# First block of a diffusion layer's projections: modulation sums on VectorE alone, side work tied behind the last convolution, value bounds by maxima

## The chip, the cores and the metric

The kernel runs on one core of a Trainium2 chip. The core has five engines with a queue each: TensorE (PE, with its weight loads as PEld), VectorE (DVE), ScalarE (ACT), GpSimd (POOL) and SyncE (SP), which issues the DMAs. Each engine works through its queue in the order in which the program was laid down. The metric is device time in microseconds: the median before is 2546.75 us (three runs, 2542.22 to 2547.43).

## The reference

One layer of a backbone works on 128 context tokens and 2048 latent tokens of width 1024. What matters here is the front part of it:

```python
def modulation(cond, w_mod_l, b_mod_l):
    m = jax.nn.silu(cond) @ w_mod_l + b_mod_l
    return jnp.split(m[:, None, :], N_MOD, axis=-1)
...
    h = rmsnorm(x, norm_mix_l) * (1.0 + sc1) + sh1
    proj = h @ w_in_l
    qkv = jax.nn.silu(centred_conv(qkv, conv_l))
    q, k, v = jnp.split(qkv, 3, axis=-1)
    q = l2norm(q.reshape(B, T, H_A, DK))
    k = l2norm(k.reshape(B, T, H_A, DK))
```

The six parts of the modulation have 1024 columns each, for two conditions (context and latent). The first two are needed at once; the others are needed after the projections. Behind this part come the delta-rule scans, the gated MLP, the output projection, the feed-forward part and the final norm.

## The kernel before

**Tiles and blocks.** The 17 token tiles of 128 are taken in six blocks: five of three tiles, the last of two. In each block twelve feature tiles are projected, in the order of four key heads (gi 1), four query heads (gi 0) and four value heads (gi 2). A feature tile is eight rows of 128 input features times three matmuls (`mm3`, lines 297 to 299), since weights and tokens are split into a high and a low half of 16 bits. `convolve` (lines 637 to 642) then makes the three-tap convolution and the silu of it: a copy on ACT (637), two multiply-adds on DVE (639), tanh on ACT (641), one more multiply-add on DVE (642). `to_tokens` transposes the result on PE (651) and takes norms on ACT (668, 672); `to_features` transposes keys back (681) and evicts them (682), `products` multiplies keys and queries (692).

**Weights and their powers.** Before a weight group may be split into halves (`split16`, ACT 205 and DVE 206), a power of two is needed that bounds its values. For the keys it comes from a maximum of absolute values on DVE (`largest`, 219). For queries and values it comes from sums of squares on ACT (`squares`, 248, with a read of the accumulator), and `group_power` then takes the maximum (253) and calls `powers`: transpose on PE (224), maximum (226), product with the identity (228), a matmul with ones that spreads it over the partitions (229), a copy (232), the power -1/2 on POOL (234) if the input was squared, a mask of the exponent (235), a scale and a reciprocal (237, 238 or 240, 241). `group_ready` scales the taps (873), and then the splits of that group can begin.

**Modulation sums.** `mods` holds the steps of the later six column groups (jc 4 to 9, eight steps each). For jc 4, `split_mod_steps` splits each fetched row block (ACT 198, DVE 199) and sums on PE with two matmuls per step against `cW` (456, 457). For the others, `mod_steps` keeps two accumulators on DVE (325 for the first step, 327 after it), and `total` adds over partitions with eight small matmuls on PE (336) and four adds (342).

**Order.** A scheduler lays the instructions down on each engine by its own estimate of when each is ready, so that a step written late may be laid down early. `behind` and `in_turn` add an order for ACT and DVE alone: the instructions of a step come after those of a named earlier step. For `mods` the named step is the modulation step before it, and at first the splits of the key weights; nothing holds them behind the convolutions that are written ahead of them. `late` does not exist yet. Side work is dealt into the feature tiles by `interleave`: splits of query weights in tiles 0 and 1, value rows `w1_raw(2, k)` in tiles 0 to 3 with their squares, value splits in tiles 4 to 7, rows and columns of the next block (`prep_block`; ACT 540 for the rows' squares, DVE 597 and 600 for the columns), and from block 2 on the rows and splits of the next weight groups.

## Time and profile before

The profiled execution took 2547.12 us, of which the span from the first to the last instruction is 2545.4 us; the 1.7 us around it are not in the trace.

| | value |
|---|---|
| median of the runs | 2546.75 us |
| the profiled execution | 2547.12 us |
| its span | 2545.4 us |
| PE busy | 2492.7 us (98%) |
| DVE busy | 1857.0 us (73%) |
| ACT busy | 1278.6 us (50%) |
| mean granted TensorE clock | 0.993 |

How to read it: a view of windows gives the busy time of each engine in a stretch, with the granted TensorE clock (1.00 is full, 0.50 half). A row of the timeline gives the start, the length, the engine, the line, the operation, what it writes and reads, how often, and in brackets the idle time before it and what ended it. Records of matmuls overlap: one of 128x388 is recorded as 0.33 us while the next starts 0.16 us after it.

### The profile page before, as it was taken

The numbers are of one execution on the slowest core, as the hardware profiler recorded it, in microseconds if no ns is written. First come the engines' busy times: TensorE is split into PE (matmuls) and PEld (weight loads), VectorE is DVE, ScalarE is ACT, GpSimd is POOL, SyncE is SP. The second block draws the span as 40 slices with busy tenths as digits, with TensorE's granted clock in tenths as the row PEclk, the third lists the DMA queues.
The fourth block names the chain that finished last, engine by engine and source line by source line (L and its number), as shares of the span: only waits on it lengthen the run. The fifth ranks groups of instructions, "written<-read, shape, count | busy, mean of one in ns | idle before, by whom it ended". The sixth has DMA issues, their size and how long they took to land.

```text
span 2545.4 us, 44002 instructions
## 1 busy us (share of the span) xinstructions
PE 2492.7 (98%) x15150; PEld 1915.7 (75%) x15150; DVE 1857.0 (73%) x3861; ACT 1278.6 (50%) x3157; POOL 237.4 (9%) x429
## 2 busy tenths in 40 slices
PE   8899999999999999999999999999999999999998
PEld 3466568566666688888888888888888888888887
DVE  4856878777777888986687877777765557784875
ACT  3765665555555667763455544444343433243442
POOL 3111223211111111210000000000000000000000
PEclk9899999999999999999999999999999999999999
DMA  8754755644444657885877789655489979786673
GB/s 284 259 179 142 223 168 174 201 148 133 140 137 148 196 175 248 289 280 174 292 235 234 247 292 336 194 174 175 140 280 375 339 251 327 252 262 205 226 262 108
DMA packets 479334, 566.61 MB, mean 223 GB/s; under 512 B 37684, under 2 KB 284764, under 8 KB 475526
## 3 DMA queue, kind: packets, MB, share of 16 engines
q1 hardware_dynamic: 479110, 563.80, 67.8%
q8 instruction: 119, 1.95, 0.3%
q14 instruction: 105, 0.86, 0.1%
HBM read 392.90 MB, written 170.76 MB: 221 GB/s over the span
## 4 chain that ended last, share of the span: by engine, by line
PE 81%; DVE 8%; DMA 6%; ACT 2%; SPq 1%; issue 1%; POOL 1%; POOLq 0%; DVEq 0%; ACTq 0%
PE f L297 16%; PE f L299 16%; PE f L298 15%; PE pj L297 6%; PE pj L298 6%; PE pj L299 6%; PE pd L1127 5%; PE pm L297 1%; PE pm L299 1%; PE pm L298 1%; PE pt L692 1%; DMA raw<-in_w_ff_dram 1%; DMA raw<-in_w_mod_dram 1%; DMA QK<-qk_d 1%; PE pt L651 1%
## 5 line engine op out<-in xcount | busy, mean ns | idle before, releaser
L297 PE MATMUL f<-hop,zH 128*128 128x512 f32 (+1 forms) x976 | 376.2, 386 | 1.2 <-ACT zH L1649 1.2
L299 PE MATMUL f<-hop,zL 128*128 128x512 f32 (+1 forms) x976 | 376.2, 386 | 0.4 <-DVE zL L1643 0.4
L298 PE MATMUL f<-hop,zH 128*128 128x512 f32 (+1 forms) x976 | 376.1, 386 | 0.0
L297 PE MATMUL f<-hop,wH 128*128 128x512 f32 x896 | 349.7, 391 | 3.0 <-DMA hop<-hop_d 1.5
L298 PE MATMUL f<-hop,wH 128*128 128x512 f32 x896 | 348.7, 389 | 0.0
L299 PE MATMUL f<-hop,wL 128*128 128x512 f32 x896 | 347.3, 389 | 0.0
L1649 ACT CAST zH<-zraw 128x512 fp32r<-128x512 f32 x240 | 146.3, 620 | 291.5 <-DMA zraw<-s_d 87.0
L1643 DVE TENSOR_TENSOR zL<-zraw,zH 128x512 fp32r<-128x512 f32 x240 | 162.5, 687 | 72.4 <-ACT zH L1649 52.7
L297 PEld LDWEIGHTS f<-hop,zH 128*128 128x128 f32 x976 | 183.3, 188 | 38.6 <-ACT zH L1649 1.8
L299 PEld LDWEIGHTS f<-hop,zL 128*128 128x128 f32 x976 | 183.3, 188 | 38.3 <-DVE zL L1643 1.3
L298 PEld LDWEIGHTS f<-hop,zH 128*128 128x128 f32 x976 | 183.3, 188 | 36.8 <-issue 0.2
L297 PEld LDWEIGHTS f<-hop,wH 128*128 128x128 f32 x896 | 168.2, 188 | 38.7 <-ACT p L1722 2.3
L299 PEld LDWEIGHTS f<-hop,wL 128*128 128x128 f32 x896 | 168.2, 188 | 35.3
L298 PEld LDWEIGHTS f<-hop,wH 128*128 128x128 f32 x896 | 168.3, 188 | 34.5
L298 PE MATMUL pj<-kL,w 128*128 128x386 f16 (+2 forms) x568 | 182.0, 323 | 0.8 <-DVE kL L600 0.7
L297 PE MATMUL pj<-kH,w 128*128 128x386 f16 (+2 forms) x568 | 181.7, 323 | 1.1 <-DVE cv L639 0.5
L299 PE MATMUL pj<-kH,w 128*128 128x386 f16 (+2 forms) x568 | 180.4, 321 | 0.0
L181 POOL TENSOR_TENSOR r<-rsq,nhalf 128x1 f32<-128x1 f32 (+1 forms) x37 | 25.3, 683 | 1388.5 <-DVE rsq L180 1388.5
L1649 ACT CAST wH<-s 128x512 fp32r<-128x512 f32 x96 | 59.4, 621 | 123.3 <-DVE s L1643 116.4
L639 DVE SCALAR_TENSOR_TENSOR cv<-pj,vec,cv 128x384 f32<-128x384 f32 (+2 forms) x142 | 83.2, 590 | 42.2 <-ACT cv L637 40.8
L297 PE MATMUL pj<-w,hrow 128*128 128x512 f16 x248 | 94.0, 379 | 0.0
L298 PE MATMUL pj<-w,hrow 128*128 128x512 f16 x248 | 94.0, 379 | 0.0
(456 smaller groups left out, 5547.2 us busy)
## 6 DMA issues: line engine op xcount, KB each, us to landing
zraw<-z_d SPq DMA_DIRECT2D x212, 256.0 KB, 4.4
raw<-in_w_ff_dram SPq DMA_DIRECT2D x192, 256.0 KB, 5.1
hop<-hop_d SPq DMA_DIRECT2D x28, 1024.0 KB, 9.6
z_d<-c SPq DMA_DIRECT2D x96, 256.0 KB, 4.7
zraw<-s_d SPq DMA_DIRECT2D x96, 256.0 KB, 5.3
raw<-in_w_mod_dram SPq DMA_DIRECT2D x80, 256.0 KB, 3.1
r<-in_w_ff_dram SPq DMA_DIRECT2D x80, 256.0 KB, 5.1
s_d<-s SPq DMA_DIRECT2D x64, 256.0 KB, 3.1
```

The source lines that it names most:

```text
L181: G.tensor_tensor(out=out, in0=t[:np_, :n], in1=nhalf[:np_, :n], op=ALU.pow)
L297: T.matmul(ps, lh, rh, start=first and i == 0, stop=False, skip_group_check=more)
L298: T.matmul(ps, lh, rl, start=False, stop=False, skip_group_check=more)
L299: T.matmul(ps, ll, rh, start=False, stop=last and i == n - 1, skip_group_check=more)
L639: V.scalar_tensor_tensor(out=cv, in0=ps[:, w : w + ncol - 2], scalar=convw[:, w, j : j + 1], in1=cv, op0=ALU.mult, op1=ALU.add)
L651: T.transpose(pq[:, i * P : (i + 1) * P], u["x2"][i], ident)
L692: T.matmul(ps[:, i * P : (i + 1) * P], kTt[:, i * P : (i + 1) * P], rhs[i], start=True, stop=True)
L1127: T.matmul(p[:, h, :], lhs[:, h, :], rhs[:, h, :], start=True, stop=True)
L1643: V.tensor_tensor(out=out, in0=a, in1=b, op=op)
L1649: A.copy(h, src)
```

## The change

Six edits:

- All 48 modulation steps are made by `mod_steps`; `split_mod_steps` and `cW` are gone. The accumulators come from the pool `p1`.
- The value rows no longer have squares on ACT: `squares` takes their largest absolute value on DVE, and `powers` for that group runs without the power on POOL. For inputs that are not squared the copy ahead of the mask is gone too, and the mask reads PSUM.
- `late` ties the ACT and DVE instructions of a step behind those of the convolution that was written last (`done["conv"]`). It is used for the value rows with their maxima, the rows of the next block, the rows of the later weight groups with their squares, and the modulation steps.
- The tables that need the first powers (lines 862 to 868 before) are written as a step behind the last column of the first block.
- Eight matmuls with ones (`keep_warm`), which stood at the start alone, are issued at two more places of the head: after the last first-half modulation output, and after the first `powers`.
- Keys of the first block are evicted on DVE, where ACT did it.

```diff
-        V.tensor_copy(ef, ps[:, P : P + n])
         if squared:
+            V.tensor_copy(ef, ps[:, P : P + n])
             G.tensor_tensor(out=ef, in0=ef, in1=nhalf[:, 0:n], op=ALU.pow)
-        V.tensor_scalar(out=e[:, 0:n], in0=e[:, 0:n], scalar1=0x7F800000, scalar2=None, op0=ALU.bitwise_and)
+        V.tensor_scalar(out=e[:, 0:n], in0=e[:, 0:n] if squared else ps[:, P : P + n].bitcast(I32), scalar1=0x7F800000,
+                        scalar2=None, op0=ALU.bitwise_and)
...
+        if gi == 2:
+            largest(phase[gi][:, k : k + 1], raw)
+            return
...
-        powers(power[:, i : i + 1], under[:, i : i + 1], top, 1, psum, True)
+        powers(power[:, i : i + 1], under[:, i : i + 1], top, 1, psum, gi != 2)
...
+        def keep_warm():
+            warm = pt()
+            for _ in range(WARM):
+                T.matmul(warm[:, 0:P], ones, ones, start=True, stop=True)
...
+                start = here()
...
+                done["conv"] = tc.nc.cur_bb.bb.instructions[start:]
...
-                (V.tensor_copy if bi else A.copy)(kTt[:, :n], pk[:, :n])
+                V.tensor_copy(kTt[:, :n], pk[:, :n])
...
-        mods = [st for jc in range(4, 10) for st in (split_mod_steps(jc) if jc == 4 else mod_steps(jc, pe))]
+        mods = [st for jc in range(4, 10) for st in mod_steps(jc, p1)]
...
         mod_out(r3, 1, a1, vec[:, 8:16], True)
+        keep_warm()
...
         powers(st3[:, 0:3], st3[:, 3:6], tops, 3, pt)
+        keep_warm()
...
+        in_turn("tables", tables, "column")
...
+        def late(f):
+            start = here()
+            f()
+            behind("conv", start, both)
...
-                done["mods"] = done["split"]
+                done["conv"] = done["split"]
...
-                    side += [lambda k=k: wv.append(w1_raw(2, k)) for k in range(2 * n, 2 * n + 2)]
+                    side += [lambda k=k: late(lambda: wv.append(w1_raw(2, k))) for k in range(2 * n, 2 * n + 2)]
...
-                        side.append(lambda w=w, k=n: load_w2(w, k))
+                        side.append(lambda w=w, k=n: late(lambda: load_w2(w, k)))
...
-                    side += [lambda f=f: in_turn("mods", f, "mods") for f in mods[:1]]
+                    side += [lambda f=f: late(f) for f in mods[:1]]
...
-                    side += nxt[1][n - 2 : n - 1] if bi == 0 and n >= 2 else nxt[1][n : n + 1] if bi else []
+                    side += [lambda f=f: late(f) for f in (nxt[1][n - 2 : n - 1] if bi == 0 and n >= 2 else
+                                                           nxt[1][n : n + 1] if bi else [])]
```

Line numbers shift with it. In the changed kernel `mm3` is 301 to 303, `convolve` 615, 617, 619 and 620, the norms of `to_tokens` 647 and 651, the transposes of token rows 564, the columns 574 and 577, the key eviction 661, a modulation step 329 and 331, its total 340 and 346; 205, 206, 219, 224 to 229 and 235 stay.

Three places show how the queues move. The first is PE at the end of the head, from the last output of the first modulation sums (431 before, 434 now) to the first projection; 224 and 229 are the transpose and the spreading matmul of `powers`, 587 or 564 the transposes of token rows. Before:

```order
L431 MATMUL pm<-ident,first 128x2 x4
L224 MATMUL pt<-ident,tops 3x128
L587 MATMUL pt<-ident,x 128x128 x3
L229 MATMUL pt<-topd,ones 128x3
L712 LDWEIGHTS abW
L712 MATMUL pm<-kH,abW 32x388
L297 LDWEIGHTS w_591
L297 MATMUL pj<-kH,w_591 128x388
```

Now:

```order
L434 MATMUL pm<-ident,first 128x2 x4
L224 MATMUL pt<-ident,tops 3x128
L382 MATMUL pt<-ones 128x128 x8
L564 MATMUL pt<-ident,x 128x128 x3
L229 MATMUL pt<-topd,ones 128x3
L301 LDWEIGHTS w_604
L301 MATMUL pj<-kH,w_604 128x388
```

Eight matmuls with ones now stand between 224 and 229, and the products with `abW` (712) have left the place.

The second is DVE in the first block at the power of the value weights, from 228 before and from 257 (the maximum that was 253) now; `acc` is an accumulator of the modulation, `x_1270` and the like are convolved tiles. Before:

```order
L228 TENSOR_SCALAR topd<-ident,top 1x1
L642 SCALAR_TENSOR_TENSOR x_1270<-x_1270,cv 128x386
L639 SCALAR_TENSOR_TENSOR cv<-pj,vec,cv 128x386
L327 SCALAR_TENSOR_TENSOR acc<-raw,scond,acc 128x512 x2
L180 TENSOR_SCALAR rsq<-ss_1035 128x3
L232 COPY tope<-pt 128x1
L639 SCALAR_TENSOR_TENSOR cv<-pj,vec,cv 128x386
L327 SCALAR_TENSOR_TENSOR acc<-raw,scond,acc 128x512 x2
L180 TENSOR_SCALAR rsq<-ss_1119 128x3
L180 TENSOR_SCALAR rsq<-xss 128x3
L235 TENSOR_SCALAR tope<-tope 128x1
L327 SCALAR_TENSOR_TENSOR acc<-raw,scond,acc 128x512
```

Now:

```order
L257 TENSOR_REDUCE topc<-sums 128x1
L661 COPY kTt<-pt 128x384
L226 TENSOR_REDUCE top<-pt 1x1
L617 SCALAR_TENSOR_TENSOR cv<-pj,vec,cv 128x386
L228 TENSOR_SCALAR topd<-ident,top 1x1
L661 COPY kTt<-pt 128x384
L617 SCALAR_TENSOR_TENSOR cv<-pj,vec,cv 128x386 x2
L235 TENSOR_SCALAR tope<-pt 128x1
L180 TENSOR_SCALAR rsq<-ss_1121 128x3
L617 SCALAR_TENSOR_TENSOR cv<-pj,vec,cv 128x386
L241 TENSOR_SCALAR scales<-tope 128x1
L620 SCALAR_TENSOR_TENSOR x_1148<-x_1148,cv 128x386
```

The modulation steps have left this stretch of the queue, and convolution work and a key eviction stand in their place.

The third is DVE at the end of the third block, where the first of the later weight groups is split (206); 600 or 577 makes the low half of the next block's columns. Before:

```order
L327 SCALAR_TENSOR_TENSOR acc<-raw,scond,acc 128x512
L206 SCALAR_TENSOR_TENSOR w_3015<-raw,scales,w_3015 128x512
L327 SCALAR_TENSOR_TENSOR acc<-raw,scond,acc 128x512
L255 TENSOR_TENSOR scales<-scales 128x1
L206 SCALAR_TENSOR_TENSOR w_3021<-raw,scales,w_3021 128x512
L206 SCALAR_TENSOR_TENSOR w_3091<-raw,scales,w_3091 128x512
L327 SCALAR_TENSOR_TENSOR acc<-raw,scond,acc 128x512
L206 SCALAR_TENSOR_TENSOR w_3097<-raw,scales,w_3097 128x512
L327 SCALAR_TENSOR_TENSOR acc<-raw,scond,acc 128x512
```

Now:

```order
L206 SCALAR_TENSOR_TENSOR w_3243<-raw,scales,w_3243 128x512
L206 SCALAR_TENSOR_TENSOR w_3249<-raw,scales,w_3249 128x512
L577 SCALAR_TENSOR_TENSOR kL<-full,b_201,kH 128x384 x2
L620 SCALAR_TENSOR_TENSOR x_3233<-x_3233,cv 128x384
L331 SCALAR_TENSOR_TENSOR acc<-raw,scond,acc 128x512 x2
L574 SCALAR_TENSOR_TENSOR full<-xT,a_200,rrow 128x384 x2
L617 SCALAR_TENSOR_TENSOR cv<-pj,vec,cv 128x384
L577 SCALAR_TENSOR_TENSOR kL<-full,b_201,kH 128x384
L617 SCALAR_TENSOR_TENSOR cv<-pj,vec,cv 128x384
L577 SCALAR_TENSOR_TENSOR kL<-full,b_201,kH 128x384
```

A modulation step is now one pair of multiply-adds (331) behind the last instruction of a convolution (620), and none stands between the splits.

## The prediction

> **What bounds the kernel now.** I read the page's slices first, then windows, then PE's waits, and last the timelines of the stretches that stood out.

> ```profile
> PE   8899999999999999999999999999999999999998
> PEclk9899999999999999999999999999999999999999
> ```

> PE is full nearly everywhere. Only the second slice (64 to 127 us) has a lower clock. So the kernel is bound by PE, and a change to the front part is worth what PE loses there. The windows say where; the columns are PE, PEld, DVE, ACT and POOL, each busy us (with its count), then clock, DMA share and GB/s.

> ```profile
> 44.00:51.00 7.00, 6.43 (x24) 3.44 (x24) 4.86 (x12) 3.62 (x8) 6.57 (x30) 0.55 0.85 301
> 72.00:81.00 9.00, 6.90 (x26) 3.49 (x27) 8.75 (x23) 6.96 (x16) 0.55 (x1) 0.81 0.66 212
> 96.00:116.00 20.00, 10.12 (x41) 5.52 (x39) 16.82 (x38) 16.13 (x46) 4.98 (x5) 0.66 1.00 320
> 264.00:273.00 9.00, 6.24 (x39) 2.52 (x38) 8.91 (x19) 8.87 (x22) 6.92 (x23) 0.81 1.04 360
> 350.00:400.00 50.00, 50.00 (x361) 34.86 (x359) 39.97 (x91) 31.53 (x101) 11.63 (x22) 1.00 0.54 154
> 700.00:2545.00 1845.00, 1817.61 (x10240) 1481.91 (x10238) 1354.29 (x2603) 860.93 (x1981) 98.28 (x121) 1.00 0.72 236
> ```

> Length less busy time times clock is what a stretch loses: 7 - 6.43 x 0.55 = 3.5 us, 9 - 6.90 x 0.81 = 3.4, 20 - 10.12 x 0.66 = 13.3, 9 - 6.24 x 0.81 = 3.9. Together 24.1 us: nearly all that this part can give. From 700 us on PE is 98.5% busy, and the queues there keep nearly their order, so time won in front should reach the end.

> The largest loss, at 96 to 116 us, is the wait for the value weights' power. PE has done its query tiles, and the chain goes (timelines of PE, ACT, DVE and POOL):

> ```profile
> 97.40 0.27 PE L224 MATMUL pt<-ident,topc 128*1 128x128 f32 x1
> 100.27 0.38 PE L229 MATMUL pt<-topd,ones 1*128 1x1 f32 x2 [2.60 <-DVE topd L228]
> 112.29 0.53 PE L297 MATMUL pj<-kH,w 128*128 128x388 f16 x1
> 94.28 0.66 ACT L248 ACTIVATE junk<-raw 128x512 bf16<-128x512 f32 x1
> 110.93 2.56 ACT L205 ACTIVATE w<-raw,scales 128x512 f16<-128x512 f32 x4
> 99.23 0.86 DVE L325 TENSOR_SCALAR acc<-raw,scond 128x512 f32<-128x512 f32 x2
> 100.02 0.20 DVE L228 TENSOR_SCALAR topd<-ident,top 1x1 f32<-1x1 f32 x1
> 101.25 1.40 DVE L327 SCALAR_TENSOR_TENSOR acc<-raw,scond,acc 128x512 f32<-128x512 f32 x2
> 103.63 0.76 POOL L234 TENSOR_TENSOR tope<-tope,nhalf 128x1 f32<-128x1 f32 x1
> 105.90 0.14 DVE L235 TENSOR_SCALAR tope<-tope 128x1 int32<-128x1 int32 x1
> 107.75 0.14 DVE L237 TENSOR_SCALAR scales<-tope 128x1 f32<-128x1 f32 x1
> 109.71 0.16 DVE L238 RECIPROCAL scales<-scales 128x1 f32<-128x1 f32 x1
> ```

> The last square begins on ACT at 94.28, the transpose (224) is at 97.40, the first value matmul at 112.29: 14.9 us. No step of the chain takes 1 us; the links stretch because DVE works in queue order, and pairs of modulation multiply-adds (325, 327) stand between them, some of which wait for their rows. The query weights took the same chain with less between its links:

> ```profile
> 70.42 0.27 PE L224 MATMUL pt<-ident,topc 128*1 128x128 f32 x1
> 77.67 0.50 PE L297 MATMUL pj<-kH,w 128*128 128x388 f16 x1
> ```

> That is 7.25 us.

> **The change part by part.** The sum is made against the profiled execution's 2547.12 us (span 2545.4 us and 1.7 around it), 0.4 us above the median.

> *A, the value power (loses 13.3).* By the queues, no modulation step is left in the chain; the copy, the power on POOL and the eight squares are gone. Eight maxima come to DVE instead, earlier in the queue. What they cost and what leaves is in the groups of 64 to 113 us and of the key maxima:

> ```profile
> L248 ACT ACTIVATE junk<-raw 128x512 bf16<-128x512 f32 x9 | 5.8, 642 | 0.0
> L248 ACT ACTIVATION_READ_ACCUMULATOR junk<-raw 128x1 f32 x9 | 1.9, 207 | 0.0
> L198 ACT CAST wH<-raw 128x512 fp32r<-128x512 f32 x8 | 4.8, 616 | 0.6 <-DMA raw<-in_w_mod_dram 0.5
> L199 DVE TENSOR_TENSOR wL<-raw,wH 128x512 fp32r<-128x512 f32 x8 | 5.4, 681 | 0.2 <-PE pm L457 0.2
> L327 DVE SCALAR_TENSOR_TENSOR acc<-raw,scond,acc 128x512 f32<-128x512 f32 x10 | 7.2, 742 | 0.0
> 34.54 2.73 DVE L219 TENSOR_REDUCE upto<-raw 128x1 f32<-128x512 f32 x4 [0.98 <-DMA raw<-in_w_in_dram]
> ```

> ACT sheds about 6.8 us of squares and reads (8 of 9) and 4.8 of casts. DVE takes 8 x 0.68 = 5.5 us of maxima and sheds 5.4 of low halves and 8.1 of accumulation (7.2, and 0.9 for 325), so the maxima are covered by what leaves; without that they would lengthen the chain by 5.5. The four key evictions, some 0.5 us each, also go from ACT to DVE, inside the chain. The transpose now stands in PE's queue ahead of the last 24 query matmuls, each 0.16 us start to start: 3.9 us of cover. If the chain takes the 7.25 us of the query weights, 3.3 us stay open; a half-clock spell after it (1.0 to 1.5 us lost) makes 4.3 to 4.8. Gain 8.5 to 9; I take 9. Ends: 4.5, if half of the present delay comes back through ACT (the first split stands behind the copy of the last query tile), and 13.3.

> [...]

> *B, the query power (loses 3.4).* The chain stays, and squares with it. Its wait now covers the 16 products with `abW` (16 x 0.16 = 2.6 us), which were spread ahead of it; but 229 stands behind them, 2.6 us after 224 where it was 1.45. Net 1.5 (0 to 3).

> *C, the head (44 to 51 us lose 3.5, of which 6.43 x 0.45 = 2.9 by the clock).*

> ```profile
> 1.24 3.78 PE L380 MATMUL pt<-ones 128*128 128x128 f32 x16 [1.24 <-DVE ones L374]
> 40.27 0.38 PE L224 MATMUL pt<-ident,tops 128*3 128x128 f32 x1 [3.64 <-DVE tops L835]
> 41.26 0.58 PE L229 MATMUL pt<-topd,ones 3*128 3x3 f32 x2
> 44.56 0.48 PE L712 MATMUL pm<-kH,abW 128*32 128x388 f16 x1 [2.72 <-POOL kH L582]
> ```

> Eight matmuls with ones took 3.78 us at the start; at twice the rate 1.9. Between 224 and 229 DVE needs only 0.6 us, so 229, and every scale and column behind it, is 1.3 to 3.2 us late. Against that stand 2.9 us of clock and 0.3 of DVE work that leaves the chain (the copy and two scalings). Net between 0 and 1.9; I take 1 (-1.5 to 2.9: also that the clock falls again in the wait behind 229, and that the head delays nothing). The other eight, near 28 us, meet a PE that soon waits for the key maxima anyway.

> *D, the end of the third block (loses 3.9).* From 250 to 290 us DVE is full:

> ```profile
> L327 DVE SCALAR_TENSOR_TENSOR acc<-raw,scond,acc 128x512 f32<-128x512 f32 x28 | 19.8, 739 | 0.0
> 265.85 0.40 PE L336 MATMUL pm<-acc,pick 128*2 128x128 f32 x8 [1.41 <-DVE acc L327]
> 205.39 0.27 PE pj L712
> 142.16 0.27 PE pj L712
> ```

> A block is 63.2 us (142.16 to 205.39, from the chain), a tile 5.3, so 40 us hold 7.6 tiles and, with a pair behind each convolution, 15 multiply-adds instead of 28: 9 us off a full engine. Gain 3.5 (0 to 3.9).

> *E, PE's own work.* The 16 split matmuls go:

> ```profile
> L457 PE MATMUL pm<-wL,cW 128*128 128x512 f32 x8 | 4.1, 514 | 1.2 <-DVE wL L199 1.2
> L456 PE MATMUL pm<-wH,cW 128*128 128x512 f32 x8 | 3.6, 456 | 0.8 <-ACT wH L198 0.8
> ```

> They start 0.22 us apart when unhindered, and about half lay in waits: 8 x 0.22 = 1.8 won. One more total (eight small matmuls, two groups of 0.40) costs 0.8. Net 1.

> *F, later blocks.* The modulation steps that ran in the first block move to blocks 2 to 6, with eight more pairs. Taking the rows of DVE's queue between the ends of four convolutions, each at the mean that its group has here, its work per four tiles peaks at about 21.5 us, an estimate, against PE's 4 x 5.3 = 21, and the last total comes 7 us of PE work ahead of the transposes that read it back through memory. From 350 to 400 us DVE was busy 39.97 of 50 and PE never waited. Cost 1.5 (0 to 6). SP's queue isn't tied: value rows still go early, and the modulation rows that stood ahead of them leave.

> Sum: 9 + 1.5 + 1 + 3.5 + 1 - 1.5 = 14.5 us. **2547.1 - 14.5 = 2532.6 us.**

> **The rivals.** *The chain hardly gets shorter.* Against ACT's relief stands that its queue still puts norms and a copy ahead of the value splits. A is 4.5 and D 2: a gain of 8.5, 2538.6 us.

> *VectorE becomes the bound in blocks 2 to 6, and the kernel is slower.* If the backlog at the ends of the blocks outgrows what the three `pj` buffers cover (two tiles, 10.5 us of PE), the loss of 264 to 273 us recurs at four ends: D is 0 and F costs 4 x 3.9 = 15.6. The sum is 9 + 1.5 + 1 + 1 - 15.6 = -3.1: 2550.2 us. For it speaks 21.5 against 21; against it, that the peaks last four to eight tiles and troughs of 12 to 15 us follow.

> [...]

> **How the numbers follow.** Forecast 0.62, chain hardly shorter 0.19, clock 0.10, VectorE bound 0.09. The range takes in the forecast's bounds and the first and third rival, up to 2545 us; its lower end, 2523, is all 24.1 us. About 0.2% (5.1 us) is what a measurement can tell from no change, so faster means below 2541.7. The forecast gives 0.60 of faster and 0.02 of the same, the short chain 0.12 and 0.07, the clock 0.10, the VectorE case 0.02 of the same and 0.07 of slower: 0.82, 0.11, 0.07.

> **What would show it.** A: the span from the second 224 of the block to the first value matmul near 7 us, with query matmuls inside it, and no modulation row on DVE before 160 us. B and C: 229 at 42.6 to 44.5 us, and a clock of 1.0 from the first projections. D: no idle PE at the turn of the third and fourth block. F: PE's waits on 331, 340 or 577 below 2 us in all. A DVE without gaps between 170 and 400 us with PE waiting on `cv` would make me wrong, and so would a loss of the gain behind 450 us.

## The result, and the profile after

The changed kernel takes **2527.19 us** (median of four runs, 2525.39 to 2528.62) against 2547.09 us (four runs, 2542.22 to 2547.54) for the kernel before: a ratio of 0.9926, interval 0.9909 to 0.9943. That is 19.9 us less. The forecast was 14.5 us less, 2532.6, with a range of 2523 to 2545. The profiled execution took 2525.39 us, of which the span is 2523.7, 21.7 us less than before. In the three later sessions the kernel before had medians of 2545.55, 2544.45 and 2544.21 us, so the size of the gain is known to some 3 us and no better.

The slices of the page, which had one weak slice before, the second:

```profile
PE   9999999999999999999999999999999999999998
PEclk9999999999999999999999999999999999999999
```

The windows of the same part (columns as in the prediction: busy us of PE, PEld, DVE, ACT and POOL with counts, then clock, DMA share, GB/s):

```profile
40.00:51.00 11.00, 8.23 (x38) 6.49 (x39) 5.39 (x19) 6.36 (x17) 4.87 (x22) 0.69 0.96 347
51.00:72.00 21.00, 19.93 (x127) 12.56 (x125) 15.00 (x39) 13.89 (x32) 6.62 (x30) 1.00 0.58 160
72.00:81.00 9.00, 7.37 (x34) 3.81 (x35) 8.92 (x22) 9.00 (x22) 1.10 (x1) 0.81 0.73 257
81.00:96.00 15.00, 13.35 (x77) 8.01 (x75) 12.26 (x32) 11.45 (x39) 3.62 (x4) 0.89 0.50 137
96.00:116.00 20.00, 20.00 (x135) 13.95 (x134) 17.72 (x33) 14.62 (x46) 1.35 (x8) 1.00 0.91 275
260.00:275.00 15.00, 15.00 (x99) 9.57 (x97) 12.86 (x27) 12.31 (x43) 3.37 (x4) 1.00 0.59 177
350.00:400.00 50.00, 48.72 (x398) 38.98 (x397) 44.91 (x107) 31.09 (x92) 5.80 (x20) 1.00 0.52 153
```

With the same sum as in the prediction (length less busy time times clock) the stretch from 96 to 116 us, which lost 13.3, loses nothing. The wait for the value power is now at 81 to 96 and loses 15 - 13.35 x 0.89 = 3.1. The stretch at 264 to 273 loses nothing either. The query power still loses 1.1 + 3.0 us (51 to 81), and 1.3 are new at 350 to 400.

The value power's wait in the timelines of PE, DVE and ACT, from the third transpose (224) to the first value matmul (98.28; the matmuls of 91.35 to 97 belong to the last query tile):

```profile
88.39 0.27 PE L224 MATMUL pt<-ident,topc 128*1 128x128 f32 x1
89.83 0.38 PE L229 MATMUL pt<-topd,ones 1*128 1x1 f32 x2 [0.51 <-DVE topd L228]
91.35 0.34 PE L301 MATMUL pj<-kH,w 128*128 128x388 f16 x1 [1.14 <-DVE tope L235]
98.28 0.33 PE L301 MATMUL pj<-kH,w 128*128 128x388 f16 x1
91.22 0.14 DVE L235 TENSOR_SCALAR tope<-pt 128x1 int32<-128x1 int32 x1
92.48 0.14 DVE L242 RECIPROCAL scales<-scales 128x1 f32<-128x1 f32 x1
93.63 5.01 ACT L205 ACTIVATE w<-raw,scales 128x512 f16<-128x512 f32 x8
```

The first value split begins 5.2 us after the transpose (before: 110.93 - 97.40 = 13.5), and the 24 query matmuls behind 229 fill nearly all that is left: PE idles 0.51 + 1.14 us. From the transpose to the first value matmul it is 9.9 us, not the 7 that I had named as a sign, with 5.6 us of query matmuls in it.

To follow the gain through the program, I take as landmarks the copies of a tile's projection on ACT (637 before, 615 now); tiles are counted from 0, twelve to a block. The same copy is at 89.4 and 88.4 us for tile 4 (the first query tile), 141.7 and 125.5 for tile 12 (the second block's first), and last:

```profile
L637 ACT ACTIVATE cv<-pj,vec x71: 452/581/637, 70.1 to 437.8; 128x384 f32<-128x384 f32 x48, 128x256 f32<-128x256 f32 x12, 128x386 f32<-128x386 f32 x11
```

```profile
L615 ACT ACTIVATE cv<-pj,vec x71: 455/580/602, 66.5 to 417.9; 128x384 f32<-128x384 f32 x48, 128x256 f32<-128x256 f32 x12, 128x386 f32<-128x386 f32 x11
```

437.8 - 417.9: in the profiled executions 19.9 us are there when the last projection is copied, and 1.8 more come behind it. That the medians differ by the same 19.9 is chance.

### The profile page after: what moved, and what is told of

It reads as the page before. It is cut to its first block, busy times and chain, and to the rows that moved or that the text cites. A ratio compares the mean times of both kernels' runs of the same rounds, so it can differ in the third digit from the quotient of the medians.

```text
span 2523.7 us, 44015 instructions
## 1 busy us (share of the span) xinstructions
PE 2482.3 (98%) x15182; PEld 1917.2 (76%) x15182; DVE 1865.2 (74%) x3877; ACT 1267.1 (50%) x3129; POOL 231.9 (9%) x428
## 4 chain that ended last, share of the span: by engine, by line
PE 84%; DVE 7%; DMA 4%; ACT 2%; issue 1%; SPq 1%; POOL 1%; POOLq 0%; DVEq 0%; ACTq 0%
PE f L301 16%; PE f L303 16%; PE f L302 16%; PE pj L301 6%; PE pj L302 6%; PE pj L303 6%; PE pd L1116 4%; DMA QK<-qk_d 2%; PE pm L301 1%; PE pm L303 1%; PE pm L302 1%; PE pt L671 1%; DMA raw<-in_w_ff_dram 1%; PE pt L630 1%; PE pm L425 1%
```

## The experiments

Theory H: what counts is the hold, that no modulation multiply-add stands in VectorE's queue ahead of the first block's convolutions and powers. Rival M: the value maxima and the lighter ScalarE shorten the chain. All twelve runs in one table: how many us ahead of the kernel before the copy of a tile is (tile 4: behind head and keys; 12: behind the value power; 29; 44: behind the third block's end; 71: last), the median of the runs and the ratio with its interval. The kernel before ran beside each, for the ratio; the entries by tiles set one profiled execution of each kernel against the one of the kernel before.

| kernel | 4 | 12 | 29 | 44 | 71 | median us | ratio |
|---|---|---|---|---|---|---|---|
| changed | 1.0 | 16.2 | 15.3 | 20.3 | 19.9 | 2527.2 | 0.9926 (0.9909 to 0.9943) |
| before_mods_held | 4.1 | 13.3 | 8.8 | 14.7 | 15.7 | 2533.5 | 0.9959 (0.9944 to 0.9974) |
| before_maxima | -0.5 | 1.5 | 1.5 | 1.0 | 0.9 | 2542.5 | 0.9991 (0.9981 to 1.0000) |
| mods_unheld | -6.4 | -11.3 | -11.1 | -3.0 | -3.8 | 2549.5 | 1.0022 (1.0013 to 1.0032) |
| squares_back | 2.8 | 12.4 | 11.2 | 16.2 | 15.8 | 2529.4 | 0.9944 (0.9926 to 0.9962) |
| fourth_split | -1.4 | 13.8 | 9.4 | 14.6 | 15.8 | 2535.1 | 0.9964 (0.9952 to 0.9975) |
| only_sums_held | -0.5 | 14.2 | 14.3 | 20.2 | 21.4 | 2529.2 | 0.9940 (0.9923 to 0.9956) |
| key_copy_on_scalar | -1.2 | 16.2 | 15.0 | 20.1 | 20.6 | 2528.3 | 0.9937 (0.9923 to 0.9951) |
| one_more_add | -0.2 | 15.0 | 15.4 | 18.7 | 15.0 | 2535.2 | 0.9963 (0.9949 to 0.9976) |
| no_extra_warm | 0.1 | 14.0 | 13.6 | 18.7 | 18.8 | 2522.7 | 0.9915 (0.9900 to 0.9930) |
| filled_waits | 4.0 | 16.7 | 16.2 | 21.2 | 21.8 | 2532.1 | 0.9949 (0.9934 to 0.9964) |
| untied_no_warm | 0.7 | 15.1 | 14.5 | 19.6 | 19.1 | 2524.7 | 0.9928 (0.9915 to 0.9942) |
| filled_again | 4.6 | 18.1 | 18.6 | 23.7 | 23.3 | 2522.3 | 0.9914 (0.9899 to 0.9930) |

Behind the last projection the profiled executions gain or lose up to 10 us more, in both directions (filled_waits 2.9 less, no_extra_warm 4.8 more, fourth_split 10.0 less), though the program there is nearly the same. So what an edit of the first part does is read from these landmarks, and the medians beside them. The landmarks scatter too: up to 75 us key_copy_on_scalar has the very queues of the changed kernel, and one_more_add and only_sums_held have its PE queue, yet at tile 4 these four entries go from -1.2 to 1.0 and at tile 12 from 14.2 to 16.2. A difference of 2 us between two rows says little.

### The hold: alone, and taken out

before_mods_held has it alone:

```diff
+        def late(f):
+            start = here()
+            f()
+            behind("conv", start, both)
...
-                done["mods"] = done["split"]
+                done["conv"] = done["split"]
...
-                    side += [lambda f=f: in_turn("mods", f, "mods") for f in mods[:1]]
+                    side += [lambda f=f: late(f) for f in mods[:1]]
```

> The kernel before with one part of the change alone: the modulation steps (the split sums of the fourth group included) tied behind the last convolution. Theory H, the hold of the modulation steps carries most: the wait of 96 to 116 us falls from 13.3 us lost to under 5 and the one of 264 to 273 from 3.9 to under 1, so 2530 to 2536 us. Rival M, the maxima on VectorE and the lighter ScalarE shorten the value chain: 96 to 116 us still loses 9 or more, only the third block's end is better, 2541 to 2546 us.

15.7 of the 19.9 us at the last copy, and 2533.5 us, as H has it; the value wait, which now begins before 96 us, still loses 7.4 us from 81 to 116 (4.8 of them behind 96), so the hold alone brings some 6 of the 10 us won there. mods_unheld takes the hold out of the changed kernel:

```diff
-                done["conv"] = done["split"]
+                done["conv"] = done["mods"] = done["split"]
...
-                    side += [lambda f=f: late(f) for f in mods[:1]]
+                    side += [lambda f=f: in_turn("mods", f, "mods") for f in mods[:1]]
```

> The changed kernel with its modulation steps tied only behind each other, as before; everything else stays. H: the waits at the value power and at the end of the third block come back, 2540 to 2552 us. M: at most 4 us slower than the changed kernel, 2527 to 2531 us.

2549.5 us, slower than the kernel before, and 23.7 us behind the changed one at the last copy. Its timelines of DVE and PE show how a modulation step costs more than its own 0.74 us:

```profile
134.46 1.41 DVE L331 SCALAR_TENSOR_TENSOR acc<-raw,scond,acc 128x512 f32<-128x512 f32 x2 [3.71 <-DMA raw<-in_w_mod_dram]
135.90 0.62 DVE L617 SCALAR_TENSOR_TENSOR cv<-pj,vec,cv 128x386 f32<-128x386 f32 x1
136.44 0.74 DVE L331 SCALAR_TENSOR_TENSOR acc<-raw,scond,acc 128x512 f32<-128x512 f32 x1
137.10 0.61 DVE L617 SCALAR_TENSOR_TENSOR cv<-pj,vec,cv 128x386 f32<-128x386 f32 x1
137.63 0.74 DVE L331 SCALAR_TENSOR_TENSOR acc<-raw,scond,acc 128x512 f32<-128x512 f32 x1
138.29 0.62 DVE L617 SCALAR_TENSOR_TENSOR cv<-pj,vec,cv 128x386 f32<-128x386 f32 x1
138.96 0.51 PE L301 MATMUL pj<-kH,w 128*128 128x388 f16 x1 [7.08 <-DVE cv L617]
```

VectorE stands 3.71 us in front of a multiply-add whose weight row isn't there, the convolutions (617) stand behind it with four multiply-adds ahead of and between them, no `pj` buffer comes free, and PE idles 7.08 us until the third 617 ends. The copies on ACT that these convolutions read were made by 131.84, so they had nothing else to wait for. M is out as the main cause.

### The value maxima

before_maxima gives the kernel before only the maxima (and no power on POOL for that group), squares_back takes them out of the changed kernel:

```diff
+        if gi == 2:
+            largest(phase[gi][:, k : k + 1], raw)
+            return
...
-        powers(power[:, i : i + 1], under[:, i : i + 1], top, 1, psum, True)
+        powers(power[:, i : i + 1], under[:, i : i + 1], top, 1, psum, gi != 2)
```

> The kernel before with only the value bounds changed: largest absolute values on VectorE, no power on GpSimd for that group. H: the modulation multiply-adds still stand in the chain and 5.5 us of maxima come on top, so 2545 to 2552 us. M: the value wait loses 5 us less or more, 2536 to 2542 us.

> The changed kernel with the value bounds again from squares on ScalarE and the power on GpSimd. H: the third transpose comes some 2 us later and the chain behind it 2 us longer, half of it behind query matmuls: 2527 to 2531 us. M: the value wait loses 6 us more or worse, 2533 us or more.

Alone they bring 0.9 us at the last copy, which is within the scatter; 2542.5 us lies between what H and M expected, and the ratio's interval ends at 1. Taken out of the changed kernel they cost 4.1 there. In squares_back the third transpose is at 93.08 instead of 88.39, behind the last query tile, and nothing is left to cover the splits (timeline of PE):

```profile
93.08 0.27 PE L224 MATMUL pt<-ident,topc 128*1 128x128 f32 x1
99.26 0.50 PE L298 MATMUL pj<-kH,w 128*128 128x388 f16 x1 [2.20 <-ACT w L205]
```

So the maxima are worth something that can be told only where the chain is free of modulation steps: they bring the transpose ahead of the last query tile.

### The fourth column group, the other holds, the key copies

fourth_split brings `split_mod_steps` and `cW` back for jc 4, held like the rest:

```diff
-        mods = [st for jc in range(4, 10) for st in mod_steps(jc, p1)]
+        mods = [st for jc in range(4, 10) for st in (split_mod_steps(jc) if jc == 4 else mod_steps(jc, p1))]
```

> The changed kernel with the fourth column group again split and summed by sixteen matmuls on PE, tied behind the last convolution like the others. If PE's own work counts in full (16 matmuls, 0.22 us each, against eight small ones): 2 to 4 us slower, 2528.5 to 2532 us. Rival, VectorE's eight pairs less in the second and third block give it back: 2525 to 2528 us.

The entry at the last copy is 4.1 us lower, but 2.4 of them are there at tiles 4 and 12, before the first split matmul at 161.08: scatter, or the making of `cW` on VectorE, which these runs don't tell apart. From tile 12 to 29, where all sixteen run, the lead falls by 4.4 us against 0.9 in the changed kernel. These 3.5 us are inside the 2 to 4 expected if PE's own work counts in full; behind tile 29 the lead grows by more than in the changed kernel, and 1.7 of them are left at the last copy. A split matmul (463 in that kernel) takes more room among projections than the 0.22 us of two of its kind in a row (71.10 to 71.32 in the kernel before):

```profile
161.05 0.33 PE L301 MATMUL pj<-kH,w 128*128 128x386 f16 x1
161.08 0.52 PE L463 MATMUL pm<-wH,cW 128*128 128x512 f32 x1
161.44 0.34 PE L302 MATMUL pj<-kL,w 128*128 128x386 f16 x1
```

From its start to the next one's is 0.36 us; 16 x 0.36 = 5.8, less 0.8 for the total that goes, is 5.0, somewhat more than the 3.5 measured. The profiled execution lost more at the turn to the scans (a wait of 3.2 us for `Y` at 450 us), which no reason of mine forecast; with a median of 2535.1 the kernel is slower than expected by 3 us.

only_sums_held takes the hold off everything but the modulation steps:

```diff
-                    side += [lambda k=k: late(lambda: wv.append(w1_raw(2, k))) for k in range(2 * n, 2 * n + 2)]
+                    side += [lambda k=k: wv.append(w1_raw(2, k)) for k in range(2 * n, 2 * n + 2)]
...
-                        side.append(lambda w=w, k=n: late(lambda: load_w2(w, k)))
+                        side.append(lambda w=w, k=n: load_w2(w, k))
```

(and likewise for the rows of the next block)

> The changed kernel with the hold kept for the modulation steps alone; value rows with their maxima, the next block's rows and the later weight rows go as early as before. If only the modulation's hold matters: within 2 us of the changed kernel, 2525 to 2529.5 us. Rival, the other holds keep VectorE and ScalarE free for convolutions: 2531 us or more.

21.4 us at the last copy against 19.9, and a median 2 us above the changed kernel's. The other holds bring nothing that can be told here.

key_copy_on_scalar:

```diff
-                V.tensor_copy(kTt[:, :n], pk[:, :n])
+                (V.tensor_copy if bi else A.copy)(kTt[:, :n], pk[:, :n])
```

> The changed kernel with the first block's keys copied out of PSUM on ScalarE again, as before. Theory: the copies are some 0.5 us each and not what the value chain waits for: within 2 us of the changed kernel, 2525 to 2529.5 us. Rival, a copy on ScalarE stands ahead of the value splits and delays them: 2530 us or more, with the clock half for more than one step at the value power.

20.6 against 19.9 at the last copy, 2528.3 us: no difference that can be told. (The step that makes the tables, with which the products with `abW` moved, has no run of its own.)

### Does VectorE set the pace in blocks 2 to 6?

one_more_add puts a multiply-add that nothing uses behind each modulation step:

```diff
-                    side += [lambda f=f: late(f) for f in mods[:1]]
+                    side += [lambda f=f: late(lambda: (f(), V.scalar_tensor_tensor(out=spare, in0=spare, scalar=1.0, in1=spare,
+                                                                                  op0=ALU.mult, op1=ALU.add))) for f in mods[:1]]
```

> The changed kernel with one more multiply-add of 128x512 on VectorE (on a spare tile, into nothing that is used) behind each of the 48 modulation steps: 48 x 0.74 = 35.5 us more work for VectorE in blocks 2 to 6. Theory, VectorE has room there (47.9 of 55 us busy from 275 to 330): 10 steps in 55 us add 7.7, just past full, so some waits appear late in the blocks: 1 to 8 us slower, 2528 to 2535 us. Rival, VectorE already sets the pace there: 20 us slower or more, 2545 us or above. If it had much more room than its busy time says: under 1 us.

4.9 us at the last copy for 35.5 us of work, and 8 us by the medians, at the upper end of what the theory said. The windows of the changed kernel and then of this one:

```profile
275.00:330.00 55.00, 55.00 (x384) 36.27 (x383) 47.88 (x101) 38.41 (x107) 14.40 (x35) 1.00 0.69 207
```

```profile
260.00:275.00 15.00, 13.09 (x85) 8.01 (x83) 13.55 (x28) 10.65 (x34) 1.56 (x2) 1.00 0.59 179
275.00:330.00 55.00, 55.00 (x376) 37.09 (x375) 51.31 (x104) 38.16 (x109) 11.07 (x37) 1.00 0.72 211
350.00:400.00 50.00, 47.82 (x370) 36.59 (x369) 49.18 (x116) 32.24 (x100) 7.59 (x21) 0.97 0.57 165
```

VectorE goes from 87% busy to 93%, 98% from 350 on, and PE waits 4.3 us in all from 150 to 450 for `cv`. The changed kernel has room there, but not for another such step in each tile.

### The matmuls with ones, and where the clock falls

no_extra_warm takes out the two extra groups:

```diff
         mod_out(r3, 1, a1, vec[:, 8:16], True)
-        keep_warm()
...
         powers(st3[:, 0:3], st3[:, 3:6], tops, 3, pt)
-        keep_warm()
```

> The changed kernel without the two extra groups of eight matmuls with ones. Theory W, between the first transpose and its spreading matmul they cost as much as they give: that matmul comes near 41 instead of 43.9 us, the first projection near 44, the clock is half for about 10 us of the head instead of 6.8; in PE's queue the value power's spreading matmul now stands behind some 18 more query matmuls, which makes the value wait up to 3 us longer; 2525 to 2531 us, and the first key convolutions 1 to 3 us earlier. Rival, they hold the clock and are worth it: the first key convolutions come later than in the changed kernel, 2530 us or more.

The first key tile is copied 5.8 us ahead of before instead of 3.6. In the changed kernel the extra matmuls stand in front of the spreading matmul (229), which DVE had made ready at 40.9 (timeline of PE):

```profile
40.08 0.27 PE L224 MATMUL pt<-ident,tops 128*3 128x128 f32 x1 [1.39 <-DVE tops L814]
40.19 3.12 PE L382 MATMUL pt<-ones 128*128 128x128 f32 x16
43.88 0.49 PE L229 MATMUL pt<-topd,ones 3*128 3x3 f32 x2
47.06 0.50 PE L301 MATMUL pj<-kH,w 128*128 128x388 f16 x2 [2.69 <-ACT w L205]
```

The kernels that differ from the changed one only behind the head have that copy 1.2 to 3.6 us ahead, so without the extra matmuls the head is 2 us earlier or more. But at tile 4 nothing of it is left (0.1 against 1.0), and at tile 12 no_extra_warm is 2.2 us behind: PE waits 2.29 us for a convolution at 92.24, and the scheduler puts 229 behind most of the last query tile, at 97.14. By the medians it is 4.5 us faster than the changed kernel, more than W expected; yet the intervals of the ratios overlap, and as it is 1.1 us behind at the last copy, that gain arises behind the projections, where the two programs are nearly the same.

The granted clock shows why the extras didn't help more. In the records of these runs it changes only in steps of 3.41 us. Windows of the changed kernel on these steps:

```profile
37.32:40.73 3.41, 1.35 (x11) 0.97 (x11) 2.93 (x12) 1.87 (x5) 0.00 (x0) 1.00 1.06 387
40.73:44.15 3.42, 3.42 (x18) 3.09 (x16) 0.19 (x1) 1.60 (x6) 0.00 (x0) 0.50 1.04 399
44.15:47.56 3.41, 0.72 (x5) 0.49 (x6) 2.80 (x12) 1.52 (x3) 1.43 (x6) 1.00 1.04 401
47.56:50.97 3.41, 3.41 (x15) 2.26 (x13) 2.04 (x5) 2.52 (x6) 3.41 (x17) 0.50 0.79 233
71.45:74.87 3.42, 1.41 (x10) 0.67 (x8) 3.34 (x13) 3.42 (x10) 0.00 (x0) 1.00 1.04 401
74.87:78.28 3.41, 3.41 (x12) 1.61 (x12) 3.41 (x7) 3.41 (x9) 0.00 (x0) 0.50 0.51 184
```

Three steps at full clock, with 2.06, 2.69 and 2.01 us of idle PE, are each followed by one at half clock in which PE works. Theory K makes a rule of that. Its bounds, 1.8 and 1.2 us, are an estimate from the six profiles before it: from 20 to 900 us the clock stayed full there after 1.75 us of idle PE at the most, and fell after 1.27 at the least. Two kernels test it by putting matmuls with ones into the waits themselves, tied behind a named matmul on PE; the last query tile is tied behind the value power's 229:

```diff
         T.matmul(ps[:, P : P + n], phase["ones"][0:n, :], d[0:n, 0:n], start=True, stop=True)
+        done["spread"] = tc.nc.cur_bb.bb.instructions[start:]
+        if "fill" in phase:
+            start = here()
+            phase["fill"](phase["count"].pop(0))
+            behind("spread", start, (mybir.EngineType.PE,))
...
-        keep_warm()
+        start = here()
+        keep_warm(5)
+        behind("spread", start, (mybir.EngineType.PE,))
...
+                if bi == 0 and n == 7:
+                    main = [lambda f=f: after_spread(f) for f in main]
```

> The changed kernel with the sixteen extra matmuls taken out and 5, 8, 6 and 4 matmuls with ones put into the waits themselves: behind the last modulation output, and behind the spreading matmul of the first, the query and the value power; the last query tile is tied behind the value power's spreading matmul, as it stands in the changed kernel anyway. Theory K, the clock of a step of 3.41 us is half where PE idled 1.8 us or more in the step before, and full where it idled under 1.2: none or one of the four half-clock steps between 40 and 96 us is left, and the head's spreading matmul comes near 41 us; 2516 to 2523 us. Rival, the clock falls for another reason, or the fillers delay what they stand ahead of: 3 or 4 half steps stay, 2524 to 2530 us.

Two of the four half steps went (those that followed the steps of 44.2 and 71.5 us), where K had none or one left and the rival three or four; the two that stayed follow steps with 2.43 and 2.14 us of idle PE, as K's rule has it. The kernel is 1.9 us further ahead than the changed one at the last copy, within the scatter. By the median, 2532.1, it is slower than either theory said: the profiled execution lost 2.9 us behind the projections, and the other three took 4 us longer still, for a reason that no trace shows. The fillers had also been too few in one place and too many in another (five ahead of the first transpose left 2.43 us idle in that step; the eight behind 229 ran at half clock and took 3.7 us). untied_no_warm has all counts at 0, filled_again 11, 6, 6 and 0:

> The changed kernel without the sixteen extra matmuls, but with the last query tile tied behind the value power's spreading matmul on PE, which keeps the place that it has in the changed kernel. Theory: it joins the head's 2 to 3 us of the kernel without the extra matmuls with the value wait of the changed one: 20 to 22.5 us ahead of the kernel before at the last convolution (the changed one 19.9, the one without the extra matmuls 18.3), 2518 to 2525 us. Rival, the tie holds PE up in front of that matmul: 18 or less, 2524 us or more.

> The kernel of the run before (no extra matmuls, last query tile tied) with fillers in three waits: 11 matmuls with ones behind the last modulation output, 6 behind the spreading matmul of the first power, 6 behind that of the query power. Theory K (half clock follows a step of 3.41 us with about 1.8 us or more of idle PE): the head keeps the full clock in the step behind the first transpose, no half step follows the query power, at most two of all half steps before 100 us are left, against four or five without fillers; 1 to 4 us further ahead at the last convolution, 2515 to 2523 us. Rival, the fillers delay what stands behind them by what the clock gives: no further ahead or behind.

Windows on the clock's steps, first of untied_no_warm, then of filled_again:

```profile
37.65:41.07 3.42, 0.13 (x1) 0.13 (x2) 3.20 (x11) 0.40 (x1) 0.00 (x0) 0.50 1.03 383
41.07:44.48 3.41, 1.45 (x6) 0.98 (x5) 2.20 (x11) 3.32 (x11) 0.22 (x1) 0.50 1.05 398
44.48:47.89 3.41, 2.67 (x11) 2.00 (x12) 1.59 (x3) 1.52 (x5) 3.39 (x21) 0.50 1.02 398
```

```profile
37.35:40.77 3.42, 2.33 (x20) 1.95 (x18) 2.99 (x11) 0.87 (x3) 0.00 (x0) 1.00 1.05 387
40.77:44.18 3.41, 2.24 (x17) 1.99 (x17) 1.89 (x10) 2.92 (x9) 1.04 (x8) 1.00 1.06 402
44.18:47.59 3.41, 2.73 (x19) 2.02 (x20) 2.31 (x5) 2.32 (x6) 3.41 (x17) 1.00 1.02 398
68.07:71.49 3.42, 1.45 (x11) 0.86 (x10) 2.87 (x11) 3.21 (x10) 0.00 (x0) 1.00 1.01 322
71.49:74.90 3.41, 3.41 (x14) 1.91 (x13) 2.48 (x5) 3.41 (x7) 0.00 (x0) 0.50 1.06 406
```

The head keeps the full clock, and filled_again is 4.2 us further ahead at the last copy than untied_no_warm (3.9 at tile 4 already), which differs from it by the fillers alone. Two half steps are left, as expected, but one of them follows the query power, which K had excluded; they stand behind steps with 1.97 and 1.23 us of idle PE. untied_no_warm fell short of its 20 to 22.5 (19.1): the tie of the last query tile brings 0.3 us there (1.1 at tile 12) and not 2. With 2522.3 us filled_again has the lowest median, with the kernel without the extras beside it; against the changed kernel's ratio the intervals overlap. That it beats the changed kernel shows at the last copy, by 3.4 us in one execution of each, and not in the whole time.

## Why the prediction was right, step by step

The mechanism was right: PE bound, the gain in the wait for the value power and at the third block's end, carried to the end. The sum was 5.4 us short by the medians; the terms missed by less and by more, in both directions, and that the total stayed near is in part luck:

- **A, the value power, +9.** By the windows 13.3 - 3.1 = 10.2. That the modulation steps in the chain were the main cause is shown by taking the hold alone and taking it out. The bound of 7.25 us taken from the query power was too long for the chain itself (5.2 us to the first split). The maxima, which I costed as covered, are worth some 4 us with the hold and 0.9 without it. The first modulation row on VectorE is at 155.9, not behind 160.
- **B, the query power, +1.5.** It failed: 3.4 lost before, 4.1 now. From the transpose to the first query matmul it takes 7.35 us (66.80 to 74.15) as it took 7.25. The 16 products with `abW` came into the wait as I had it, but nine split matmuls that PE had done there before (and a tenth right behind it) left the wait, and I had left out that the wait then idles.
- **C, the head, +1.** 229 came at 43.88, inside the forecast 42.6 to 44.5. The clock was to be 1.0 from the first projections; it fell again, from 47.6 to 51.0, after a wait of 2.69 us behind 229. Without the extra matmuls the first key tile is 2.2 us earlier: up to there they cost more than the term's lower end, -1.5, and its sign was wrong. By tile 4 the difference is gone.
- **D, the third block's end, +3.5.** The 3.9 us of that stretch are gone; from tile 29 to 44 the lead grows by 5.0.
- **E, PE's own work, +1.** The mis-sized term. Up to the last copy PE idles 437.8 - 413.85 = 23.95 us before and 417.9 - 406.02 = 11.88 now; the half-clock steps cost it half of its busy time in them (in the changed kernel matmuls of 128x388 start 0.32 us apart in the step from 74.87, at 75.24 and 75.56, and 0.16 behind it, at 78.55 and 78.71), 10.3 us before and 6.8 now. Of the 19.9 us that makes 12.1 of idle time and 3.5 of clock, and leaves 4.3 of work; without the extra matmuls with ones it would be some 7 (an estimate: 16 records took 3.12 at half clock, and there are 32 more). I had counted 8 split matmuls at 0.22 us, less 0.8 for the total. All sixteen, at 0.22 to 0.36, are 2.7 to 5.0 less that total; those in the query power's wait come back as the loss in B. And I had nothing for the 16 products with `abW`: before, they stand one by one or in pairs among projections, mostly with 0.26 to 0.27 us from one start to the next on both sides; now they follow one another at 0.16. At 0.1 us for each of some two dozen such changes that is 2 to 3 us, an estimate; no run moved these products alone.
- **F, later blocks, -1.5.** From tile 12 to 29 the lead falls by 0.9 and from 44 to 71 by 0.4: 1.3 together. No wait on 331, 340 or 577 is left; the 1.28 us that PE waits at 382.6 are for `absb`.

The products with `abW` in the timelines of PE, before and now:

```profile
68.13 0.34 PE L712 MATMUL pm<-kH,abW 128*32 128x388 f16 x1
68.40 0.50 PE L297 MATMUL pj<-kH,w 128*128 128x388 f16 x2
```

```profile
67.18 0.33 PE L692 MATMUL pm<-kL,abW 128*32 128x388 f16 x1
67.34 0.33 PE L691 MATMUL pm<-kH,abW 128*32 128x388 f16 x1
```

By the landmarks: 1.0 (up to tile 4), 15.2, -0.9, 5.0, -0.4. The 15.2 are not all won there: when the first query tile is copied, PE has begun 200 matmuls of projections in the changed kernel and 187 before, so it is 2.1 us further on than the copies show (13 at 0.16). Of the rivals, the short chain and the VectorE case didn't come; one_more_add shows that the second of them was one modulation-sized step per tile away. The clock case is wrong too. No run shows that short gaps cost no clock: in the changed kernel it fell four times with no gap above 2.69 us, once with none above 1.14.

What stays open: why the turn to the scans (435 to 470 us) and the scans from 870 to 1150 us give or take some us with kernels that differ only in front. In the second of these the changed kernel waits 5.2 us in six waits for `Y` from ACT, the one without the extras 0.9, in a program that is nearly the same there (PE's waits from 960 to 1160, of the changed kernel and of no_extra_warm):

```profile
PE pd L1196 <- ACT Y L1212: 4.2, 5, 1.4
PE pd L1228 <- ACT Y L1212: 1.0, 1, 1.0
```

```profile
PE pd L1194 <- ACT Y L1210: 0.9, 2, 0.4
```

## What to carry to other kernels

Side work that waits for its own data must not be queued on an engine ahead of work that PE's buffers depend on: in mods_unheld one late weight row, with four multiply-adds of 0.74 us ahead of and between convolutions, cost 7 us of PE. A tie to the work that it should follow costs a few lines, and only with it was the earlier transpose worth more than the scatter (4.1 us at the last copy against 0.9). Matmuls that keep the clock up belong behind the last step that the wait's chain needs of PE, in a number that fits the wait: with fillers in three waits filled_again was 4.2 us ahead of untied_no_warm at the last copy. In front of that step they lengthen the chain: the first spreading matmul came at 43.88 in the changed kernel and at 41.00 in filled_again. Matmuls of another shape took PE less time in a row than one by one among projections here: the products with `abW` start 0.16 us apart in a row and 0.26 to 0.27 among projections, the split matmuls 0.22 and 0.36.

## What the runs showed of the hardware

```profile
76.78 0.50 PE L456 MATMUL pm<-wH,cW 128*128 128x512 f32 x1 [0.83 <-ACT wH L198]
78.00:80.00 2.00, 2.00 (x7) 0.92 (x6) 2.00 (x5) 2.00 (x6) 0.00 (x0) 0.50 0.94 291
```

Why the number of gaps should matter is open. A half step costs up to 3.41 x 0.5 = 1.7 us of PE's work, an estimate from its length and the clock: the kernel before had nine half steps in the first part, the changed one four, filled_again two.
